# A hybrid S5 / HGRN2 block on one core: another order of weight slices, other head starts, and squares spread over 14 steps

## The chip, the cores and the metric

The kernel runs on one core of a Trainium2 chip (the other seven are idle). The metric is the device time of one execution in microseconds. Three executions of the kernel before took 1543.37, 1548.42 and 1546.52 us, median 1546.52.

## The reference

One decoder block over x of 2048 x 1024 (float32). All of it is one normalised projection, two token mixers, gates and an output projection:

```
xn   = rms_norm(x, norm_w)
proj = xn @ w_in
u_a, z_a, q_b, f_b, i_b, og_b, z_b, g_a, g_b = split(proj)
y_a  = s5_branch(u_a, z_a, ...)
y_b  = hgrn2_branch(q_b, f_b, i_b, og_b, z_b, lower_bound, norm_w)
merged = sigmoid(g_a) * (y_a @ w_proj_a) + sigmoid(g_b) * (y_b @ w_proj_b)
return rms_norm(x + merged @ w_out, final_norm_w)
```

In the HGRN2 branch a head has 128 channels: q goes through silu, f through a sigmoid with a lower bound (the forget gate), key = 1 - forget, and the recurrence is evaluated in chunks, as scores inside a chunk and a carried state between chunks. So a head can start only when its columns of q, f, i (here V) and og (here O) of the projection are complete.

## The kernel before, in words

**Two halves, Strassen products.** The rows are worked on in two halves of 1024 (a = 0 and 1), each in two blocks of 512 columns (b). The first slices are multiplied plainly (`plain`). Then `strassen(0, s0)`, the first long stage, works through 18 slices of w_in, each 256 features wide. A slice takes seven products instead of eight. One product is 12 matmuls of 128x512: four k blocks, each as high x high, low x high and high x low part (lines 445, 446, 447), because each float32 operand is split into two parts (`split`: line 119 on ScalarE makes the high part, line 120 on VectorE the low part). In the code a product is one `yield`, here called a step. The order of the steps is (i,0), then products 5 and 6 of the slice before, then (i,1) to (i,4): the last product of slice i is step 7i+7 (the very first has no predecessor). Steps are counted from 0; there are 126.

**What lies beside the steps.** `w_ops` fetches the weights of a product three steps ahead, splits them and stores the split parts to DRAM (wc) for the second half. When a block of a slice is complete its evacuation runs: `snap` copies an accumulator to SBUF on ScalarE (line 451), `total` adds another to it on VectorE (line 454). qf slices give Q and F of a head (`qf_evac`), vo slices V and O (transposed on TensorE by `turn`), zb and za slices a silu, ga and gb slices a sigmoid.

**Events.** `timed` runs a list of (step, function) pairs between the steps. `heads(a, first, every, last)` makes the events of the four heads: `hgrn_core` of a head is stepped 22 times from its start on, two blocks b alternating over 11 stages (`hgrn_block`), then a Newton iteration for the norm, then `hgrn_fin`. Its first stage makes K, KX = K*Q, the parts kh and kl, and two matmuls against ones (lines 953 and 954); stages 1 to 8 double the width of the chunk, then follow the states (st, pv) and the outputs (po). In the first half the heads start at steps 3, 38, 73 and 108, the last one with its 22 steps squeezed into 18.

**Row sums of the second half.** `norm_stats(1, b)` loads four tiles xr of 128x1024 and squares each on ScalarE with a running sum (line 191), then `newton_rsqrt` (12 small VectorE instructions) and `norm_diag` (four VectorE instructions) make a diagonal; `bcast(b)` broadcasts it by a matmul. `stats(0)` is an event at step 2, `stats(1)` one at step 8, the broadcasts are at 13 and 18. `xprep(1, k)` (36 pieces from step 20 on) prepares the X operands of the second half and stores them to DRAM.

**After the 126 steps** comes `merge_b(0)`, 20 more steps, with four loads of the w_proj_b weights (rpb, line 304; parts hpb and lpb), and then `strassen(1, s1)`, the second long stage.

**What sets the order.** TensorE's order is the order in which the code is written (`manual_schedule`). The order on ScalarE (ACT), VectorE (DVE) and in SyncE's DMA queue (SP) is set by a scheduler from the written program. Each engine works its list from front to back: an instruction that waits holds all behind it on that engine.

Of the kernel before, what the change touches and what calls it, by code (L numbers as in the profile page):

```python
# [11 lines left out]
F32 = mybir.dt.float32  # L12
# [3 lines left out]
AF = mybir.ActivationFunctionType  # L16
ALU = mybir.AluOpType
# [4 lines left out]
D = 1024  # L22
HALF = 1024
# [8 lines left out]
def hybrid_block(  # L32
# [24 lines left out]
    nc = tc.nc  # L57
    V = nc.vector
# [41 lines left out]
    def y4(name):  # L100
        return yp.tile([128, 1024], F32, name=name, tag="y")
# [13 lines left out]
    def r2(name, dt=F32R):  # L115
        return rp.tile([128, 512], dt, name=name, tag="r")
# [61 lines left out]
    def norm_stats(a, b):  # L178
        t0 = a * HALF + b * 512
        c0 = a * 8 + b * 4  # L180
        for i in range(4):
            rows = slice(t0 + i * 128, t0 + (i + 1) * 128)
            if a == 0:
                for h in range(2):
                    xr = r2(f"xr{a}{b}{i}{h}", F32)
                    nc.sync.dma_start(xr, xn[rows, h * 512 : h * 512 + 512])
                    S.activation(xr, xr, AF.Square, accum_out=ssh[:, h * 4 + i : h * 4 + i + 1])
            else:
                xr = y4(f"xr{a}{b}{i}")
                nc.sync.dma_start(xr, xn[rows, :])  # L190
                S.activation(xr, xr, AF.Square, accum_out=ssx[:, c0 + i : c0 + i + 1])
        if a == 0:
            V.tensor_tensor(ssx[:, c0 : c0 + 4], ssh[:, 0:4], ssh[:, 4:8], op=ALU.add)
        newton_rsqrt(ssx[:, c0 : c0 + 4], 4, 1.0 / D, rst[:, c0 : c0 + 4])

    def norm_diag(a, b):
        c0 = a * 8 + b * 4
# [1144 lines left out]
    def step(g, n=1):  # L1342
        for _ in range(n):
            next(g, None)
# [9 lines left out]
        for _, f in ev[i:]:  # L1354
            f()

    def heads(a, first, every=35, last=22):
        ev = []
        cores = [hgrn_core(a, h) for h in range(4)]
        fins = [hgrn_fin(a, h, None if a or h < 3 else (lambda b, y: yb_pair(a, 3, b, y))) for h in range(4)]  # L1360
        for h in range(4):
            t0 = first + every * h
            n = last if h == 3 else 22
            for s in range(22):
                ev.append((t0 + s * n // 22, lambda c=cores[h]: step(c)))
            ev.append((t0 + n - 1, lambda c=cores[h]: run(c)))
            for s in (-8 if a == 0 and h == 3 else 0, 1, 2, 3, 4):
                ev.append((t0 + n + s, lambda f=fins[h]: step(f)))
            ev.append((t0 + n + 4, lambda f=fins[h]: run(f)))
        return ev  # L1370

    def steps(ev, g, at):
        for t in at:
            ev.append((t, lambda: step(g)))
        ev.append((at[-1], lambda: run(g)))
# [10 lines left out]
    with tc.manual_schedule(engines={mybir.EngineType.PE}):  # L1386
# [37 lines left out]
        for i in range(12):  # L1424
            step(g)
            step(x0p[i // 4], 3 if i % 4 == 1 else 2)
            if i % 4 == 3:
                run(x0p[i // 4])
        run(g)
        s0 = [zz(0, "zb", 0), gt(0, 0, 0), gt(0, 1, 0), qf(0, 1), vo(0, 1), zz(0, "zb", 1), gt(0, 0, 1), gt(0, 1, 1),  # L1430
              qf(0, 2), vo(0, 2), zz(0, "za", 0), gt(0, 0, 2), gt(0, 1, 2), qf(0, 3), vo(0, 3), zz(0, "za", 1),
              gt(0, 0, 3), gt(0, 1, 3)]
        d0 = strassen(0, s0)
        g = plain(SL_VO, 1, w_vo, e_vo)
        step(g, 1)
# [10 lines left out]
        def bcast(b):  # L1446
            rb1[b] = norm_bcast(1, b, dg1[b])
# [1 line left out]
        dg1 = {}  # L1449

        def stats(b):
            norm_stats(1, b)
            dg1[b] = norm_diag(1, b)

        ev = heads(0, 3, 35, 18)
        ev += [(2, lambda: stats(0)), (8, lambda: stats(1)), (13, lambda: bcast(0)), (18, lambda: bcast(1))]
        xg = chain(*[xprep(1, k, rb1) for k in range(4)])
        steps(ev, xg, [20 + (s * 92) // 35 for s in range(36)])
        for i in range(6):
# [11 lines left out]
        d1 = strassen(1, s1)  # L1471
        step(d1)

        ev = heads(1, 17)
        bg_ = ssm_build()
        steps(ev, bg_, [8 + (s * 50) // 42 for s in range(43)])
        batches = [ssm_batch(0, b, wr4, wr4) for b in range(8)] + [ssm_batch(1, b, wr4, wr4) for b in range(2)]
# [134 lines left out]
```

## Time and profile before

| | before |
|---|---|
| three runs, median | 1546.52 us (1543.37 to 1548.42) |
| the profiled execution's own time | 1544.01 us |
| its span in the trace | 1542.2 us |
| mean granted TensorE clock | 0.984 |
| TensorE busy | 1467.2 us, 95% of the span |
| VectorE busy | 1099.2 us, 71% |
| ScalarE busy | 636.3 us, 41% |
| first long stage, steps 0 to 125 | 103.67 to about 534 us |
| merge_b(0), then start of the second long stage | about 534 to 587; from 588 us |

How to read it: a step of 12 matmuls that follow each other without a gap takes 2.72 us from start to start (0.227 us each), though the profile gives each matmul 0.39 us, since neighbours overlap. Head work on TensorE comes on top. At half of the clock the matmuls stand 0.43 us apart. A step's time in the trace is from its first matmul to that of the next step; a wait shows as a step that is longer than its instructions.

### The profile page before, as it was taken

To read this page: it belongs to the slowest core of one execution; us is meant where nothing else is said; L and a number is where in the kernel's file an instruction comes from. 1 tells how busy PE (TensorE), PEld (TensorE's weight loads), DVE (VectorE), ACT (ScalarE), POOL (GpSimd) and SP (SyncE) were. 2 spreads that over 40 slices of the span, in tenths; PEclk is the share of its full clock that TensorE was granted. 3 is DMA by queue.
4 is the path that set the end of the run, shared out by engine and by line. 5 is a ranking of instruction groups with operands and counts; after the bars stand their busy time and mean duration, and the time that the engine had idled before them with its cause. 6 is when DMAs were issued, how large, how long until landed. Compare 5 with 4: busy or idle time off the path is not lost.

```text
span 1542.2 us, 21503 instructions
## 1 busy us (share of the span) xinstructions
PE 1467.2 (95%) x7360; PEld 1206.0 (78%) x7360; DVE 1099.2 (71%) x2403; ACT 636.3 (41%) x1385; POOL 3.6 (0%) x24
## 2 busy tenths in 40 slices
PE   7997999999999989989999999999989899999997
PEld 5776788888878768868777888788768788778886
DVE  5898788788788635975665877766648977765445
ACT  7455555554554513223322445333344333532222
POOL 0000000000000000000000000000000000000000
PEclk9998999999999999999999999999989999999999
DMA  9639779887978896586669559678976963854602
GB/s 336 174 121 301 296 274 337 328 293 270 352 271 324 288 371 219 183 208 216 221 205 318 176 148 296 225 254 261 321 223 205 302 208 128 277 187 133 211 14 103
DMA packets 202141, 369.23 MB, mean 239 GB/s; under 512 B 66800, under 2 KB 76016, under 8 KB 202032
## 3 DMA queue, kind: packets, MB, share of 16 engines
q1 hardware_dynamic: 173872, 342.69, 65.8%
q10 hardware_dynamic: 28160, 25.17, 4.8%
q8 instruction: 58, 0.95, 0.3%
q14 instruction: 51, 0.42, 0.1%
HBM read 221.51 MB, written 146.28 MB: 238 GB/s over the span
## 4 chain that ended last, share of the span: by engine, by line
PE 64%; DMA 15%; DVE 14%; ACT 3%; issue 3%; SPq 1%; ACTq 0%; DVEq 0%
PE pd L445 12%; PE pd L447 12%; PE pd L446 12%; PE pf L1259 3%; PE pf L1258 3%; PE pf L1260 3%; DMA rw<-in_wi_dram 3%; PE pp L1097 2%; PE pp L1098 2%; PE pp L1096 2%; PE sc L966 1%; DMA w<-wc 1%; DVE w L120 1%; DMA y_d<-T 1%; PE pd L342 1%
## 5 line engine op out<-in xcount | busy, mean ns | idle before, releaser
L119 ACT ACTIVATE w<-rw 128x512 fp32r<-128x512 f32 x110 | 68.5, 628 | 94.4 <-PE pd L447 45.5
L1258 PE MATMUL pf<-ho,mh 128*128 128x512 f32 x256 | 100.6, 393 | 4.5 <-ACT mh L119 4.5
L1260 PE MATMUL pf<-ho,ml 128*128 128x512 f32 x256 | 100.0, 391 | 0.2 <-DVE ml L120 0.2
L1259 PE MATMUL pf<-lo,mh 128*128 128x512 f32 x256 | 99.9, 390 | 0.0
L451 ACT ACTIVATE u<-pd 128x512 f32<-128x512 f32 x80 | 47.6, 595 | 101.0 <-PE pd L447 97.2
L120 DVE TENSOR_TENSOR w<-rw,w 128x512 fp32r<-128x512 f32 x110 | 75.2, 686 | 19.5 <-ACT w L119 19.2
L454 DVE TENSOR_TENSOR u<-u,pd 128x512 f32<-128x512 f32 x80 | 54.9, 686 | 28.8 <-PE pd L447 22.0
L342 PE MATMUL pd<-xh,hw 128*128 128x512 f32 x128 | 52.4, 409 | 9.0 <-ACT hw L119 7.5
L1258 PEld LDWEIGHTS pf<-ho,mh 128*128 128x128 f32 x256 | 48.2, 188 | 14.6 <-ACT mh L119 4.9
L1260 PEld LDWEIGHTS pf<-ho,ml 128*128 128x128 f32 x256 | 48.1, 188 | 10.8 <-DVE ml L120 0.9
L1259 PEld LDWEIGHTS pf<-lo,mh 128*128 128x128 f32 x256 | 48.2, 188 | 9.7
L119 ACT ACTIVATE mh<-sgl 128x512 fp32r<-128x512 f32 x32 | 20.1, 630 | 84.9 <-DVE sgl L1204 84.9
L343 PE MATMUL pd<-xl,hw 128*128 128x512 f32 x128 | 51.0, 398 | 0.0
L344 PE MATMUL pd<-xh,lw 128*128 128x512 f32 x128 | 50.8, 397 | 0.0
L1097 PE MATMUL pp<-yl,hpa 128*128 128x512 f32 x128 | 49.9, 390 | 0.2 <-DVE yl L120 0.2
L1096 PE MATMUL pp<-yh,hpa 128*128 128x512 f32 x128 | 50.1, 392 | 0.0
L1098 PE MATMUL pp<-yh,lpa 128*128 128x512 f32 x128 | 49.8, 389 | 0.0
L1203 DVE TENSOR_TENSOR sgl<-sgl,pp 128x512 f32<-128x512 f32 x48 | 32.8, 684 | 23.3 <-PE pp L1098 23.2
L961 ACT ACTIVATE KX<-K 128x128 f32<-128x128 f32 x128 | 32.4, 304 | 38.8 <-DVE K L1004 30.1
L967 DVE COPY_PREDICATED s_buf<-masks,sc 128x256 f32<-128x256 uint8 x64 | 32.5, 508 | 20.9 <-PE sc L966 20.9
L966 PEld LDWEIGHTS sc<-Q,KX 128*128 128x128 f32 x256 | 38.5, 191 | 9.7 <-issue 3.6
L966 PE MATMUL sc<-Q,KX 128*128 128x128 f32 x256 | 39.4, 277 | 4.1 <-DVE Q L1003 3.2
(915 smaller groups left out, 4434.5 us busy)
## 6 DMA issues: line engine op xcount, KB each, us to landing
wc<-w SPq DMA_DIRECT2D x126, 512.0 KB, 3.5
w<-wc SPq DMA_DIRECT2D x126, 512.0 KB, 4.7
rw<-in_wi_dram SPq DMA_DIRECT2D x44, 512.0 KB, 5.3
sgl<-sg_d SPq DMA_DIRECT2D x48, 256.0 KB, 3.0
sg_d<-u ACTq DMA_DIRECT2D x32, 256.0 KB, 3.3
ro<-in_wo_dram SPq DMA_DIRECT2D x16, 512.0 KB, 5.2
hh<-in_xn_dram SPq DMA_DIRECT2D x32, 256.0 KB, 5.0
out_dram<-hh SPq DMA_DIRECT2D x32, 256.0 KB, 2.4
```

What stands on the lines that cost most here:

```text
L119: S.activation(hi, raw, AF.Copy)
L120: V.tensor_tensor(lo, raw, hi.bitcast(F32), op=ALU.subtract)
L445: mm(o, w[:, 0, k], xh, start=(first and k == 0), stop=False, skip_group_check=True)
L446: mm(o, w[:, 0, k], xl, start=False, stop=False, skip_group_check=True)
L447: mm(o, w[:, 1, k], xh, start=False, stop=(k == 3), skip_group_check=True)
L966: mm(ps[:, :, c, :], ch(kx, c), qp, start=True, stop=True)
L1096: mm(ps, hi[:, k, fs], yh, start=(k == 0), stop=False)
L1097: mm(ps, hi[:, k, fs], yl, start=False, stop=False)
L1098: mm(ps, lo[:, k, fs], yh, start=False, stop=(k == last))
L1258: mm(o, mh[:, ts_], hi, start=(kk == 0), stop=False)
L1259: mm(o, mh[:, ts_], lo, start=False, stop=False)
L1260: mm(o, ml[:, ts_], hi, start=False, stop=(kk == 7))
```

## The change

Three parts. (1) The squares of the second half's rows leave `stats` and become a generator `norm_stats1`, called at steps 1, 2, 4, 5, 7, 8, 10, 11, 13 and 14: call i issues load i and squares the tile that was loaded two calls before. `stats(b)` keeps only the Newton iteration and the diagonal, at steps 9 and 15 instead of 2 and 8; the broadcasts are at 12 and 18 instead of 13 and 18. (2) The slices of the first long stage stand in another order: the qf and vo slices of heads 1, 2 and 3 end later (for qf at steps 42, 70 and 98 instead of 28, 63 and 98), the za slices go to the end, zb(1) and the gates come forward. (3) `heads` takes its starts as a list; the heads of the first half start at steps 9, 43, 71 and 100 instead of 3, 38, 73 and 108, each over 22 steps. In the second half they stay at 17, 52, 87 and 122.

```
@@ -180,18 +180,23 @@
-            if a == 0:
...
-            else:
-                xr = y4(f"xr{a}{b}{i}")
-                nc.sync.dma_start(xr, xn[rows, :])
-                S.activation(xr, xr, AF.Square, accum_out=ssx[:, c0 + i : c0 + i + 1])
...
+    def norm_stats1():
+        tiles = {}
+        for i in range(10):
+            if i >= 2:
+                xr = tiles.pop(i - 2)
+                S.activation(xr, xr, AF.Square, accum_out=ssx[:, 6 + i : 7 + i])
+            if i < 8:
+                tiles[i] = y4(f"xr1{i}")
+                nc.sync.dma_start(tiles[i], xn[HALF + i * 128 : HALF + i * 128 + 128, :])
+            yield
@@ -1354,15 +1359,15 @@
-    def heads(a, first, every=35, last=22):
+    def heads(a, starts):
...
-            t0 = first + every * h
-            n = last if h == 3 else 22
+            t0 = starts[h]
+            n = 22
             for s in range(22):
-                ev.append((t0 + s * n // 22, lambda c=cores[h]: step(c)))
+                ev.append((t0 + s, lambda c=cores[h]: step(c)))
@@ -1427,9 +1432,9 @@
-        s0 = [zz(0, "zb", 0), gt(0, 0, 0), gt(0, 1, 0), qf(0, 1), vo(0, 1), zz(0, "zb", 1), gt(0, 0, 1), gt(0, 1, 1),
-              qf(0, 2), vo(0, 2), zz(0, "za", 0), gt(0, 0, 2), gt(0, 1, 2), qf(0, 3), vo(0, 3), zz(0, "za", 1),
-              gt(0, 0, 3), gt(0, 1, 3)]
+        s0 = [zz(0, "zb", 0), gt(0, 0, 0), gt(0, 1, 0), zz(0, "zb", 1), gt(0, 0, 1), qf(0, 1), vo(0, 1), gt(0, 1, 1),
+              gt(0, 0, 2), qf(0, 2), vo(0, 2), gt(0, 1, 2), gt(0, 0, 3), qf(0, 3), vo(0, 3), zz(0, "za", 0),
+              zz(0, "za", 1), gt(0, 1, 3)]
@@ -1449,11 +1454,13 @@
         def stats(b):
-            norm_stats(1, b)
+            c0 = 8 + b * 4
+            newton_rsqrt(ssx[:, c0 : c0 + 4], 4, 1.0 / D, rst[:, c0 : c0 + 4])
             dg1[b] = norm_diag(1, b)
 
-        ev = heads(0, 3, 35, 18)
-        ev += [(2, lambda: stats(0)), (8, lambda: stats(1)), (13, lambda: bcast(0)), (18, lambda: bcast(1))]
+        ev = heads(0, (9, 43, 71, 100))
+        steps(ev, norm_stats1(), [1, 2, 4, 5, 7, 8, 10, 11, 13, 14])
+        ev += [(9, lambda: stats(0)), (12, lambda: bcast(0)), (15, lambda: stats(1)), (18, lambda: bcast(1))]
@@ -1471,7 +1478,7 @@
-        ev = heads(1, 17)
+        ev = heads(1, (17, 52, 87, 122))
```

In the changed program line numbers are 5 higher from line 186 on (7 or 8 higher behind `norm_stats1`'s end in `heads` and after it).

**First place: ScalarE's list between the start of the first long stage and its fourth step.** xr are the tiles to be squared, u_10 the copy of the first slice's accumulator after its third product, V and O the transposed head-0 values. Before:

```order
L119 ACTIVATE X036h<-xb_1123 128x512
L191 ACTIVATE xr_1276,ssx<-xr_1276 128x1024
L901 ACTIVATE V_1354<-pt_1349 128x512
L191 ACTIVATE xr_1279,ssx<-xr_1279 128x1024
L119 ACTIVATE kh_1336<-KX_1334 128x256
L961 ACTIVATE KX_1334<-K_1332 128x64x2 x2
L119 ACTIVATE w_14_1_1427<-rw_14_1_1423 128x512
L119 ACTIVATE kh_1373<-KX_1371 128x256
L904 ACTIVATE O_1391<-pt_1386 128x512
L191 ACTIVATE xr_1282,ssx<-xr_1282 128x1024
L191 ACTIVATE xr_1285,ssx<-xr_1285 128x1024
L961 ACTIVATE KX_1371<-K_1369 128x64x2 x2
```

The next row there is the copy u_10_1330. With the change:

```order
L850 ACTIVATE ezb_1274<-s_10_1251 128x512
L119 ACTIVATE X036h<-xb_1123 128x512
L456 ACTIVATE u_10_1305<-pd_10_0_1238 128x512
L909 ACTIVATE O_1343<-pt_1338 128x512
L119 ACTIVATE w_14_1_1371<-rw_14_1_1367 128x512
L195 ACTIVATE xr_1253,ssx<-xr_1253 128x1024
L456 ACTIVATE u_10_1357<-pd_10_0_1238 128x512
L195 ACTIVATE xr_1278,ssx<-xr_1278 128x1024
```

The copy u_10 stood behind four squares and two conversions of head 0; now it stands ahead of the first square, and head 0's rows are gone from this stretch.

**Second place: the start of head 1 on VectorE.** K, KX, kl are head 1's, F its forget gate, Q its query, u_3 the accumulator of its qf slice to which the last product (pd_3_3) is added. Before:

```order
L925 TENSOR_SCALAR K_2480<-F_2204 128x512
L454 TENSOR_TENSOR u_3_2075<-u_3_2075,pd_3_3_2107 128x512
L1069 TENSOR_TENSOR zy_2122<-zy_2122,py_2233 128x512
L120 TENSOR_TENSOR w_11_0_2275<-rw_11_0_2273,w_11_0_2275 128x512
L877 TENSOR_TENSOR Q_2230<-Q_2230,u_3_2075 128x512
L120 TENSOR_TENSOR X103l<-xa_1936,X103h 128x512
L454 TENSOR_TENSOR s_7_2175<-s_7_2175,pd_7_1_2245 128x512
L120 TENSOR_TENSOR w_7_5_2293<-rw_7_1_2153,w_7_5_2293 128x512
L931 TENSOR_TENSOR KX_2482<-K_2480,Q_2034 128x512
L925 TENSOR_SCALAR K_2517<-F_2145 128x512
L992 TENSOR_TENSOR Q_2034<-Q_2034,F_2204 128x512
L120 TENSOR_TENSOR kl_2485<-KX_2482,kh_2484 128x512
```

With the change:

```order
L886 TENSOR_SCALAR F_2555<-F_2555,lbp 128x512
L120 TENSOR_TENSOR w_7_4_2603<-rw_7_0_2442,w_7_4_2603 128x512
L930 TENSOR_SCALAR K_2579<-F_2555 128x512
L930 TENSOR_SCALAR K_2622<-F_2505 128x512
L936 TENSOR_TENSOR KX_2581<-K_2579,Q_2432 128x512
L459 TENSOR_TENSOR u_3_2460<-u_3_2460,pd_3_3_2473 128x512
L997 TENSOR_TENSOR Q_2432<-Q_2432,F_2555 128x512
L120 TENSOR_TENSOR kl_2584<-KX_2581,kh_2583 128x512
```

and on TensorE, with the last matmuls of that product (step 42) ahead:

```order
L450 MATMUL pd_3_3_2473<-X036h,w_3_6_2486 128x512
L451 MATMUL pd_3_3_2473<-X036l,w_3_6_2486 128x512
L452 MATMUL pd_3_3_2473<-X036h,w_3_6_2486 128x512
L958 MATMUL sc_0_2587<-kh_2583,ones_r 128x512
L959 MATMUL sc_0_2587<-kl_2584,ones_r 128x512
```

Before, ten steps lay between the slice's last product and the head's first matmul; now the matmul follows the product directly, and on VectorE the addition of that product stands between KX and kl.

**Third place: SyncE's queue in merge_b(0).** rpb_5678 is the fourth load of w_proj_b, X1.. are the X operands of the second half, sgb and mb_d the gates and results of the merge. Before:

```order
L294 DMA X114h<-xo_d_1_133 128x512
L294 DMA X114l<-xo_d_1_133 128x512
L1108 DMA sgb_5657<-sg_d_13_157 128x512
L1130 DMA mb_d_3_211<-sgb_5611 128x512
L294 DMA X124h<-xo_d_2_134 128x512
L294 DMA X124l<-xo_d_2_134 128x512
L304 DMA rpb_5678<-in_wp_dram 128x1024
```

With the change:

```order
L309 DMA rpb_5530<-in_wp_dram 128x1024
L383 DMA wc_6_5063<-w_21_6_5344 128x1024
L309 DMA rpb_5584<-in_wp_dram 128x1024
L1094 DMA yl_5338<-yb_d_2_202 128x512
L1094 DMA yl_5366<-yb_d_2_202 128x512
L309 DMA rpb_5678<-in_wp_dram 128x1024
L299 DMA X100h<-xo_d_0_116 128x512
```

The fourth load stood behind 38 loads of X operands; now it stands ahead of the first of them.

## Rows read from the trace of the kernel before

**Rows 1.** The page: busy time of each engine, and the granted clock in 40 slices

```profile
PE 1467.2 (95%) x7360; PEld 1206.0 (78%) x7360; DVE 1099.2 (71%) x2403; ACT 636.3 (41%) x1385; POOL 3.6 (0%) x24
...
PEclk9998999999999999999999999999989999999999
```

**Rows 2.** Busy PE, PEld, DVE, ACT, POOL by stretch; then granted clock, DMA share, GB/s

```profile
100.00:120.00 20.00, 14.41 (x60) 10.99 (x60) 20.00 (x34) 11.47 (x21) 0.00 (x0) 0.95 0.56 181
120.00:140.00 20.00, 14.03 (x54) 11.19 (x54) 14.74 (x41) 12.17 (x27) 0.00 (x0) 0.80 0.89 311
140.00:240.00 100.00, 100.00 (x531) 82.29 (x530) 78.97 (x180) 55.16 (x130) 0.00 (x0) 1.00 0.81 294
```

**Rows 3.** Timeline of PE, steps 2 to 5: start, duration, [idle before <- releaser]

```profile
109.71 0.50 PE L445 MATMUL pd<-X002h,w 128*128 128x512 f32 x1 [0.43 <-ACT s L451]
...
118.45 0.79 PE L954 MATMUL sc<-kl,ones_r 128*128 128x512 f32 x1 [4.52 <-DVE kl L120]
...
130.37 0.79 PE L445 MATMUL pd<-X004h,w 128*128 128x512 f32 x1 [5.97 <-ACT u L451]
...
135.59 0.40 PE L445 MATMUL pd<-X000h,w 128*128 128x512 f32 x1
```

**Rows 4.** Timeline of DVE, 117 to 130 us

```profile
117.71 0.68 DVE L120 TENSOR_TENSOR kl<-KX,kh 128x512 fp32r<-128x512 f32 x1
...
121.33 0.42 DVE L941 TENSOR_TENSOR KX<-K,Q 128x256 f32<-128x256 f32 x1
121.67 0.68 DVE L387 TENSOR_TENSOR s<-rw,rw 128x512 f32<-128x512 f32 x1
...
129.66 0.17 DVE L156 TENSOR_SCALAR smi<-small 128x4 int32<-128x4 int32 x1
```

**Rows 5.** Timeline of ACT, 118 to 130 us

```profile
118.88 1.06 ACT L191 ACTIVATE xr<-xr 128x1024 f32<-128x1024 f32 x1 [2.90 <-DMA xr<-in_xn_dram]
...
128.28 1.06 ACT L191 ACTIVATE xr<-xr 128x1024 f32<-128x1024 f32 x1 [1.38 <-DMA xr<-in_xn_dram]
...
129.74 0.58 ACT L451 ACTIVATE u<-pd 128x512 f32<-128x512 f32 x1
```

**Rows 6.** Timeline of DVE at the preparation of head 1, 216 to 223 us

```profile
216.41 0.68 DVE L454 TENSOR_TENSOR u<-u,pd 128x512 f32<-128x512 f32 x1
...
222.16 0.68 DVE L120 TENSOR_TENSOR kl<-KX,kh 128x512 fp32r<-128x512 f32 x1
222.76 0.68 DVE L931 TENSOR_TENSOR KX<-K,Q 128x512 f32<-128x512 f32 x1
```

**Rows 7.** Timeline of PE, the first matmul of head 1 that reads kl

```profile
242.72 0.39 PE L954 MATMUL sc<-kl,ones_r 128*128 128x512 f32 x1
```

**Rows 8.** Timeline of PE in merge_b(0)

```profile
569.25 0.39 PE L1098 MATMUL pb<-Y031h,lpb 128*128 128x512 f32 x1
573.76 0.80 PE L1096 MATMUL pb<-Y000h,hpb 128*128 128x512 f32 x1 [4.12 <-ACT hpb L119]
...
578.80 0.39 PE L1097 MATMUL pb<-Y030l,hpb 128*128 128x512 f32 x1
```

**Rows 9.** Timeline of ACT in merge_b(0)

```profile
572.65 1.06 ACT L119 ACTIVATE hpb<-rpb 128x1024 fp32r<-128x1024 f32 x1 [27.63 <-DMA rpb<-in_wp_dram]
```

**Rows 10.** Timeline of SP's DMA issues in merge_b(0)

```profile
566.49 0.33 SPq L304 DMA_DIRECT2D rpb<-in_wp_dram  x1
```

**Rows 11.** Timeline of PE at the start of the second long stage

```profile
601.64 0.50 PE L445 MATMUL pd<-X100h,w 128*128 128x512 f32 x1 [0.45 <-ACT w L119]
```

**Rows 12.** Timeline of ACT at the start of the second long stage

```profile
604.15 0.63 ACT L880 ACTIVATE F<-u 128x512 f32<-128x512 f32 x1 [0.51 <-DVE u L454]
```

**Rows 13.** Timeline of PE after two waits in the second long stage

```profile
811.15 0.50 PE L445 MATMUL pd<-X106h,w 128*128 128x512 f32 x1 [2.27 <-DMA w<-wc]
...
987.86 1.35 PE L1068 MATMUL py<-ident,ys 128*128 128x128 f32 x4 [2.05 <-ACT ys L1064]
...
990.29 0.63 PE L445 MATMUL pd<-X115h,w 128*128 128x512 f32 x1
```

More of the change, by code (lines that the diff above doesn't have):

```diff
@@ L182, in norm_stats @@
             rows = slice(t0 + i * 128, t0 + (i + 1) * 128)
-            if a == 0:
[L184 to L187, printed above, removed]
-            else:
-                xr = y4(f"xr{a}{b}{i}")
-                nc.sync.dma_start(xr, xn[rows, :])
-                S.activation(xr, xr, AF.Square, accum_out=ssx[:, c0 + i : c0 + i + 1])
-        if a == 0:
-            V.tensor_tensor(ssx[:, c0 : c0 + 4], ssh[:, 0:4], ssh[:, 4:8], op=ALU.add)
-        newton_rsqrt(ssx[:, c0 : c0 + 4], 4, 1.0 / D, rst[:, c0 : c0 + 4])
+            for h in range(2):
+                xr = r2(f"xr{a}{b}{i}{h}", F32)
+                nc.sync.dma_start(xr, xn[rows, h * 512 : h * 512 + 512])
+                S.activation(xr, xr, AF.Square, accum_out=ssh[:, h * 4 + i : h * 4 + i + 1])
+        V.tensor_tensor(ssx[:, c0 : c0 + 4], ssh[:, 0:4], ssh[:, 4:8], op=ALU.add)
+        newton_rsqrt(ssx[:, c0 : c0 + 4], 4, 1.0 / D, rst[:, c0 : c0 + 4])
+    def norm_stats1():
[8 more added lines that the diff above has]
+            yield
     def norm_diag(a, b):
```

## The prediction

> **What bounds the kernel now.** First the page: TensorE (PE) is busy for 1467.2 of 1542.2 us and its granted clock is near full [rows 1]. So the end moves only by what makes PE wait, or run at half clock, and every part of the change has to be priced as such a wait. The table of stretches then shows where PE waits near the change: 14.41 of 20 us busy from 100 to 120 us and 14.03 of 20 at a clock of 0.80 from 120 to 140, but 100 of 100 from 140 to 240 [rows 2]. DVE, on the other hand, has not a free moment from 100 to 120 us (20.00 of 20). The timeline of PE names the waits: steps 2 to 4 start at 109.71 us, step 5 at 135.59; inside lie an idle time of 4.52 us for kl of head 0 and one of 5.97 us for the copy u of the first slice's accumulator, and half-speed matmuls behind both [rows 3]. DVE writes that kl only from 117.71 on [rows 4]. ACT copies u at 129.74, after four squares of xr tiles that hold up its list until their loads land (2.90 and 1.38 us idle ahead of two of them) [rows 5]. So the early wait has two owners: head 0's first instructions in a full DVE list, and the squares ahead of the copy in ACT's list. The change moves both.
>
> **The change part by part.** I sum against the profiled execution (1544.01 us), which lies 2.5 us under the median of the runs, 1546.52; the result is put on the median. A measurement of this kernel can tell about 0.3%, that is 4.6 us, from no change.
>
> *The early stall goes.* Steps 2, 3 and 4 take 135.59 - 109.71 = 25.88 us [rows 3]. Their 36 matmuls at 0.227 us are 8.2 us, and the head work among them (two pairs of 128x512, one of 128x256, eight transposes) 2.0, so 10.2 without waits: 15.7 are lost. With the change head 0 starts at step 9, and kl and kh leave this stretch; the copy u stands ahead of the first square. A wait of some 0.9 us for a late X operand in step 2 stays: -14.8. The squares cost 8 times 1.06 us of ACT as before, two to three steps after their load, and ACT is idle for nearly half of this stretch (11.47 and 12.17 of 20 us busy, rows 2). If the DVE list, which is full until 120 us, makes the next weights late instead, part of it comes back: -10 at worst, -15.7 at best.
>
> *Step 12.* Head 0 now runs its first stages at steps 9 to 12 together with a gate's sum. In DVE's list twenty instructions stand between the result of head 0's stage 1 and the low part of w_18_0, the first weight of step 12: eight masks and products of 128x256 with 0.34 us from start to start [rows 4], one sum of 128x512 with 0.60 [rows 6] and eleven short ones of 0.17 busy, about 0.2 from start to start [rows 4]: 2.7 + 0.6 + 2.2 = 5.5, with w_18_0 itself 6.1 us, and 0.2 for the hand-overs. In that time PE has one step of 2.72 and its small matmuls, some 3.3 us. That is a new wait of 3.0, and step 15, whose weight is loaded behind a wc store, adds some 1.0: +4.0. Ends: +1 (if DVE reaches these rows while PE is still at an earlier step) and +5.5.
>
> *Head starts 1 to 3.* Before, the first matmul that reads kl of head 1 is at 242.72 us, and kl was begun at 222.16 [rows 6, 7]: 20 us of slack. Now it follows the last product of its own slice. When that product ends, DVE does the sum u_3, then Q*F, then kl, 0.60 us each from start to start [rows 6], and 0.1 to 0.2 for each hand-over from PE to DVE and back; head 1's kl is there some 2.3 us late, and the second block's waits again for 0.45: 2.75. Head 2 starts one step behind its slice as well (70 and 71): 2.75. Head 3 has two steps (98 and 100): 1.4. Sum +6.9. Ends: +2, if kl is made ahead of the sum and the wait is hidden, and +11, if two more splits at 0.60 and a sigmoid at 0.63 [rows 6, 12] stand in front each time.
>
> *Small waits.* Stages of head 0 that share one PSUM buffer (st, po, py) now fall in with xprep's pieces at steps 28 and 32, and the last head's, no longer squeezed, in the steps before the merge. I count +3.4 for the new ones, and -1.1 for the wait on head 3's output in the merge, which its earlier end removes: +2.3, from 0 to +4.5.
>
> *The merge.* PE ends one group of matmuls at 569.25 and starts the next at 573.76, 4.12 us idle for hpb, then runs at half clock to 578.80 [rows 8]. The eleven matmuls up to there would take 2.5 us and took 5.0; with the idle time that is 6.6 us. ACT made hpb at 572.65 after 27.63 us of waiting for the load rpb [rows 9], which SP issued only at 566.49 [rows 10]. Now the load stands ahead of 38 others, and this wait goes. But DVE's list in the merge has two splits of the next stage's weights (w_2_1, w_2_2) ahead of the product that frees PE's next accumulator, and these wait for a buffer that a later tile frees: I count 2.7 for that. Net -3.9, from -6.6 to -1.
>
> *The start of the second long stage.* ACT copies u_2_5959 and makes F from it ahead of splitting w_6_0, the weight that PE needs for the next step; before, w_6_0 came first and PE was idle for 0.45 us [rows 11]. The copy has to wait for the product; then it takes 0.58, F 0.63 [rows 5, 12], the two parts of w_6_0 0.6 each, with the hand-overs 2.7 us: +2.3, from 0 to +2.9.
>
> *The clock.* New waits of 2 to 3 us may be followed by half clock. After 2.27 us idle at 811.15 the next matmul lasts 0.50, as at full clock; after 2.05 us at 987.86 the matmuls are at 0.63, the lower of the two levels, 1.2 instead of 2.4 GHz [rows 13]. So both occur at the same length of wait. A piece of eight matmuls at 0.43 instead of 0.227 us from start to start costs 1.6 to 1.7 more. I take one of the five or six new waits: +1.7, from 0 to +6.8.
>
> The Trainium skill, page "TensorE: Matmul & The Clock Gate", section "HAM oscillation — how this bites in real kernels", says that only longer idle gaps make TensorE restart at the low clock; by it the new waits would cost their own length alone and the sum would be 1.7 lower. The trace disagrees at 987.86 [rows 13], so the rows decide.
>
> Sum: -14.8 + 4.0 + 6.9 + 2.3 - 3.9 + 2.3 + 1.7 = **-1.5 us**, on the median **1545 us**. The early stall is not saved but spread: over head starts, step 12 and the start of the second stage.
>
> **The rivals.** *A: the new waits are mostly hidden.* If DVE and ACT reach the head starts with their lists empty (ACT is idle for over half of the span, rows 1), kl is made in the gap after the product and costs 2 instead of 6.9; step 12 costs 2 instead of 4 and the clock stays up. -14.8 + 2 + 2 + 2.3 - 3.9 + 2.3 = -10.1: 1536. For it: no wait at all in 100 us after the early stall, with DVE at 79% [rows 2]. Against it: the head's matmul directly behind the product cannot start before three DVE instructions.
>
> *B: the head starts cost more (slower).* Place: sc of heads 1 to 3. Each costs the 2.75 us, two other 0.60 us splits that DVE fits in ahead of kl, and a stretch of half clock (1.7): 5.7 each, 17 together, in place of 6.9 and 1.7. Sum +6.9: 1553. It decides from 4.9 us a start on, where the sum passes +4.6. For it: DVE's list is dense in the first stage (78.97 of 100 us, rows 2), and a 2 us wait is enough for the lower clock [rows 13]. Against it: the order shows only the sum between KX and kl.
>
> *C: the early stall moves instead of going.* DVE has no free time until 120 us [rows 2]; if the weight splits of steps 5 to 8, not kl, then become what PE waits for, only 7 of the 14.8 are saved: sum +6.3, 1553. Against it: those splits ran at their places while PE waited for kl and u, not for them.
>
> **How the numbers follow.** Forecast (near balance, 1541 to 1550): 0.42. A: 0.32. B: 0.19. C: 0.07. So faster by over 0.3% 0.32, within 0.3% 0.42, slower 0.26. The ends of the terms are independent; together they are about 7.5 us either way. The range 1535 to 1555 takes in A, B and C at their own values and leaves 2 in 10 to the ends beyond.
>
> **What would show it.** Right: steps 2 to 4 in about 11 us and step 5 near 121 us; no wait for kl of head 0; idle times of 2 to 3 us ahead of the sc matmuls of heads 1 and 2 (releaser DVE kl), one of about 3 at step 12 (DVE w), none for hpb in the merge, and 2 to 3 us for a weight at the start of the second stage. A shows as head starts without idle time; B as starts at 5 us with 0.63 us matmuls behind them; C as waits for w between 120 and 135 us. The later stages, whose lists have the same order, should only shift; a difference there would prove the whole account wrong.

## The result and the profile after

The changed kernel takes 1553.67 us in the median of 8 runs (1550.03 to 1558.86), the kernel before 1544.71 (8 runs, 1542.5 to 1549.89): a ratio of 1.0059, interval [1.0042, 1.0076]. It is 9 us slower, where 1.5 us faster was forecast; the size is that of rival B. The profiled execution of the change took 1550.96 us with a span of 1549.1, 6.9 more than before.

The page of the change (busy time of each engine, then the granted clock in 40 slices) answers to [rows 1] and shows nothing: the engines do the same work, PE is busy for 2.8 us more, and the rest of its longer span (6.9 us) is waiting.

```profile
PE 1470.0 (95%) x7360; PEld 1206.7 (78%) x7360; DVE 1100.1 (71%) x2403; ACT 638.7 (41%) x1385; POOL 3.9 (0%) x24
...
PEclk9999999999999999999999999999999999999999
```

The timeline of PE in the change has the first matmuls of steps 2, 3, 4 and 5 here, which answer to [rows 3] (line numbers are higher than before, as the changed program is longer):

```profile
110.67 0.50 PE L450 MATMUL pd<-X002h,w 128*128 128x512 f32 x1 [0.79 <-ACT s L456]
...
114.87 0.48 PE L450 MATMUL pd<-X003h,w 128*128 128x512 f32 x1
...
118.06 0.48 PE L450 MATMUL pd<-X004h,w 128*128 128x512 f32 x1
...
120.92 0.39 PE L450 MATMUL pd<-X000h,w 128*128 128x512 f32 x1
```

Steps 2 to 4 take 10.25 us instead of 25.88: the early stall is gone, as forecast. Further on in the same timeline stand the waits that PE has instead:

```profile
144.91 0.50 PE L450 MATMUL pd<-X000h,w 128*128 128x512 f32 x1 [2.45 <-ACT w L119]
...
250.03 0.50 PE L958 MATMUL sc<-kh,ones_r 128*128 128x512 f32 x1 [1.68 <-ACT kh L119]
251.17 0.50 PE L959 MATMUL sc<-kl,ones_r 128*128 128x512 f32 x1 [0.64 <-DVE kl L120]
...
322.15 0.71 PE L1038 MATMUL po<-V,s_buf 128*128 128x128 f32 x4 [2.87 <-DVE st L1030]
...
351.46 0.49 PE L958 MATMUL sc<-kh,ones_r 128*128 128x512 f32 x1 [1.29 <-ACT kh L119]
352.45 0.50 PE L959 MATMUL sc<-kl,ones_r 128*128 128x512 f32 x1 [0.50 <-DVE kl L120]
...
435.76 1.35 PE L1073 MATMUL py<-ident,ys 128*128 128x128 f32 x4 [1.98 <-ACT ys L1069]
...
580.31 0.47 PE L1101 MATMUL pb<-Y000h,hpb 128*128 128x512 f32 x1 [2.51 <-DVE sgb L1134]
...
611.12 0.79 PE L450 MATMUL pd<-X100h,w 128*128 128x512 f32 x1 [6.05 <-ACT w L119]
611.71 0.63 PE L451 MATMUL pd<-X100l,w 128*128 128x512 f32 x1
```

After five of these waits TensorE runs at its lower clock for a piece, after the one at 580.31 it does not. The table of stretches shows it in the granted clock (the number behind the busy times; 0.50 is the lower of the two levels):

```profile
146.40:148.90 2.50, 2.50 (x7) 1.96 (x6) 0.69 (x3) 1.58 (x4) 0.00 (x0) 0.50 0.91 364
252.10:255.00 2.90, 2.90 (x8) 2.29 (x7) 2.71 (x5) 0.63 (x1) 0.00 (x0) 0.50 0.85 300
324.60:326.60 2.00, 2.00 (x6) 1.60 (x5) 0.45 (x1) 1.28 (x8) 0.00 (x0) 0.50 1.06 404
437.40:439.40 2.00, 2.00 (x6) 1.58 (x5) 1.50 (x3) 0.87 (x3) 0.00 (x0) 0.50 0.87 341
611.80:616.00 4.20, 4.20 (x12) 3.28 (x11) 4.20 (x10) 1.46 (x3) 0.00 (x0) 0.50 0.00 0
580.50:584.00 3.50, 3.50 (x16) 2.87 (x16) 1.55 (x3) 0.00 (x0) 0.00 (x0) 1.00 1.00 332
```

Three of the waits were forecast with nearly their size: step 12 (144.91), the starts of heads 1 and 2 (250 and 351), the merge (580.31; the wait for hpb of [rows 8] is gone). Three were not, or not in their size: po of head 1 at step 62, py of head 2 at step 94, and 6 us at the start of the second long stage, where [rows 11] had 0.45.

What is behind po stands in DVE's timeline. The state products st, which PE waits for, lie between scalings of xb (xprep), and the first of these waits 3.24 us for its load:

```profile
314.10 1.11 DVE L1030 SCALAR_TENSOR_TENSOR st<-st,t,pv 128x128 f32<-128x128 f32 x3
318.45 0.75 DVE L253 SCALAR_TENSOR_TENSOR xb<-xb,nw_t,rb 128x512 f32<-128x512 f32 x1 [3.24 <-DMA xb<-in_xt_dram]
319.12 0.34 DVE L1030 SCALAR_TENSOR_TENSOR st<-st,t,pv 128x128 f32<-128x128 f32 x1
```

At py the timeline shows the same with another load: ahead of the Newton rows, which py needs, DVE waits for a weight. (This one is read from the timeline alone; no run takes that load away.)

```profile
429.34 0.69 DVE L392 TENSOR_TENSOR s<-rw,rw 128x512 f32<-128x512 f32 x1 [3.01 <-DMA rw<-in_wi_dram]
429.95 0.17 DVE L155 TENSOR_SCALAR small<-ssq 128x8 f32<-128x8 f32 x1
```

At the start of the second long stage it is ACT that waits for a load (first row: the copy u, then F, then the split of the weight), and SP issued that load at 604.35, behind the last of the X operands; before, at 594.91 (last row, of the kernel before). Counted from the merge's first matmul that is 60.1 us after and 60.5 us before: the load comes when it always came, and PE, which no longer waits for hpb, now waits here.

```profile
605.11 0.60 ACT L456 ACTIVATE u<-pd 128x512 f32<-128x512 f32 x1 [4.84 <-PE pd L452]
606.46 0.63 ACT L885 ACTIVATE F<-u 128x512 f32<-128x512 f32 x1 [0.76 <-DVE u L459]
610.44 2.19 ACT L119 ACTIVATE w<-rw 128x512 fp32r<-128x512 f32 x4 [3.35 <-DMA rw<-in_wi_dram]
```

```profile
604.35 1.01 SPq L375 DMA_DIRECT2D rw<-in_wi_dram  x2
```

```profile
594.91 0.99 SPq L370 DMA_DIRECT2D rw<-in_wi_dram  x2
```

The account of the profiled executions, each stretch between the starts of first matmuls (step 0, step 5, the merge, the first that reads X106, the last of the program):

| stretch | before | after | difference | forecast |
|---|---|---|---|---|
| step 0 to 5 | 31.91 | 16.63 | -15.3 | -14.8 |
| step 5 to the merge | 398.81 | 423.33 | +24.5 | +16.0 |
| the merge to X106 | 73.11 | 75.20 | +2.1 | -2.7 |
| X106 to the end | 926.47 | 921.44 | -5.0 | 0 |

(The forecast of the second row is 4.0 + 6.9 + 3.4 + 1.7, of the third -1.1 - 3.9 + 2.3.) The miss has its place: steps 5 to the merge. Some 2 of its 24.5 us are no loss: six matmuls of head 0 have moved there from the stretch above (74 matmuls before, 68 after) and eight of head 3 from the one below (284 and 276).

### The profile page after: what moved, and what is told of

Read it like the earlier page. It is cut to its first block, busy times and chain, and to the rows that moved or that the text cites. A ratio compares the mean times of both kernels' runs of the same rounds, so it can differ in the third digit from the quotient of the medians.

```text
span 1549.1 us, 21472 instructions
## 1 busy us (share of the span) xinstructions
PE 1470.0 (95%) x7360; PEld 1206.7 (78%) x7360; DVE 1100.1 (71%) x2403; ACT 638.7 (41%) x1385; POOL 3.9 (0%) x24
## 4 chain that ended last, share of the span: by engine, by line
PE 61%; DVE 19%; DMA 13%; ACT 3%; issue 3%; SPq 1%; ACTq 0%; DVEq 0%
PE pd L450 11%; PE pd L452 11%; PE pd L451 11%; PE pf L1263 3%; PE pf L1265 3%; PE pf L1264 3%; PE pp L1102 2%; PE pp L1103 2%; PE pp L1101 2%; DMA rw<-in_wi_dram 2%; DVE w L120 2%; DMA y_d<-T 1%; PE sc L971 1%; DMA xb<-in_xt_dram 1%; DMA yy<-y_d 1%
## 5 line engine op out<-in xcount | busy, mean ns | idle before, releaser
L1008 DVE TENSOR_TENSOR Q<-Q,t 128x256 f32<-128x256 f32 x96 | 40.7, 424 | 8.1 <-PE sc L983 8.1
```

## The experiments

Unless said otherwise an experiment is the changed kernel with the edit shown. Times are medians, ratios are to the kernel before; stretches are read as in the table above.

### Which part does what

**Squares alone.** `s0` and the heads as before, (3, 38, 73, 108) with the last in 18 steps; part 1 stays.

```
-        ev = heads(0, (9, 43, 71, 100))
+        ev = heads(0, (3, 38, 73, 108), 18)
```

> Part 1 alone: squares spread over 14 steps, stats at 9 and 15; slices and head starts as before. Theory (T): in the trace of before, PE waited 6.1 us for the copy u behind the squares and 4.7 us for kl of head 0 behind a full VectorE list; only the first goes here, with its piece at half clock, and nothing new is paid: 1536 to 1540 us. Rival (R): the whole early gain comes from starting head 0 at step 9, and the spread squares only move the wait: within 3 us of before (1542 to 1548).

1536.61 us, 0.9931 [0.9908, 0.9955]. Steps 0 to 5 take 23.47 us: PE still waits for kl of head 0 (first fence), and not for u. From step 5 to the merge it is 400.42, as before. So part 1 alone is worth 10 us. (The profiled execution, 1541.50 us, is the slowest of the six.)

```profile
118.56 0.79 PE L959 MATMUL sc<-kl,ones_r 128*128 128x512 f32 x1 [4.51 <-DVE kl L120]
```

**Squares back.** Slices and heads of the change, squares in two bunches.

```
+            for i in range(4):
+                xr = y4(f"xr1{b}{i}")
+                nc.sync.dma_start(xr, xn[r0 : r0 + 128, :])
+                S.activation(xr, xr, AF.Square, accum_out=ssx[:, c0 + i : c0 + i + 1])
...
-        steps(ev, norm_stats1(), [1, 2, 4, 5, 7, 8, 10, 11, 13, 14])
```

> Parts 2 and 3 without part 1: squares in two bunches of four in stats at steps 2 and 8, broadcasts at 13 and 18; slices and heads as in the change. T: the copy u waits behind the squares again (about 6 us and a piece of half clock, 1.7), the kl wait does not come back: 1559 to 1563 us. R (the gain is head 0's alone): within 3 us of the change, 1550 to 1556 us.

1564.49 us, 1.0120 [1.0099, 1.0141]. The wait for u comes back, and larger, since head 0 no longer shares it out (12.86 us instead of 5.97, and no wait for kl). Steps 0 to 5 take 31.46 us, as before: head 0's move gains nothing while the squares hold the copy.

```profile
130.48 0.80 PE L450 MATMUL pd<-X004h,w 128*128 128x512 f32 x1 [12.86 <-ACT u L456]
```

**Old slices, new heads.** Parts 1 and 3, `s0` as before.

> Parts 1 and 3, the slices in the order of before: heads at 9, 43, 71 and 100, but qf1 and qf2 end at steps 28 and 63 instead of 42 and 70. T: the early gain stays, the idle times for kl at heads 1 and 2 (2.75 and 2.2 us, with one piece of half clock behind) are gone, head 3's (slack of two steps as in the change) stays: 1544 to 1549 us. R: the price lies in where the heads fall against the other events (waits at steps 62 and 94, start of the second long stage), not in the slack to the slices: 1551 to 1556 us.

1555.44 us, 1.0063 [1.0040, 1.0085]; step 5 to the merge 420.19. No start wait is left at heads 1 and 2, and hardly anything is gained: 3 us of 423.33. Other waits stand there (py of head 0 at 221.15, step 32, 2.29 us, which all runs with the old slices and head 0 at step 9 have and the runs with the new order have not; po at 318.40, pv at 412.35 and 513.86 us, 2 to 3 us each), the po and the first pv with DVE waiting for a load in front, the last behind a load that ACT and DVE wait for at 508.34:

```profile
315.17 0.75 DVE L253 SCALAR_TENSOR_TENSOR xb<-xb,nw_t,rb 128x512 f32<-128x512 f32 x1 [2.57 <-DMA xb<-in_xt_dram]
...
403.49 0.69 DVE L392 TENSOR_TENSOR s<-rw,rw 128x512 f32<-128x512 f32 x1 [1.87 <-DMA rw<-in_wi_dram]
...
409.56 0.75 DVE L253 SCALAR_TENSOR_TENSOR xa<-xa,nw_t,rb 128x512 f32<-128x512 f32 x1 [2.05 <-DMA xa<-in_xt_dram]
```

(That a head needs all four of q, f, V and O to start, as said at the beginning, is too strict: with the new slices the last product of head 1's vo slice is step 49, six steps after its start. With the old slices it is step 35, and the wait at po is there all the same.)

**Heads three steps later.**

```
-        ev = heads(0, (9, 43, 71, 100))
+        ev = heads(0, (9, 46, 74, 103))
```

> The change with heads 1 to 3 three steps later (9, 46, 74, 103), slices as in the change. T: no idle time ahead of the first sc matmul of heads 1 to 3, 5 to 7 us less than the change if nothing else moves: 1546 to 1550 us. R: the waits at steps 62 and 94 only move with the heads and others take the place of those gone: 1551 to 1556 us.

1534.49 us, 0.9923 [0.9904, 0.9943]: 19 us less than the change for one tuple of numbers, three times what either expectation allowed. Step 5 to the merge falls from 423.33 to 402.78. The waits at the starts, at po (step 62) and at py (step 94) are all gone, with one of 1.18 us for po of head 1 at step 66 in their place; the wait for hpb in the merge (5.02 us) is back, the one at the second long stage is gone.

**Old slices, heads three steps later.** Both edits.

> Slices in the order of before, heads at 9, 46, 74 and 103 (three steps later than in the change). P (the place of the heads against loads and other events decides): like the run with those heads and the new slices, 1532 to 1538 us. L (the new slice order is what profits from later heads, since with the old slices the loose starts gained nothing): 1548 to 1556 us.

1537.19 us, 0.9950 [0.9930, 0.9969]; step 5 to the merge 405.84. With either order of slices the heads at 46, 74, 103 give about 404 and at 43, 71, 100 about 422. The slice order by itself is worth 3 us, for one set of starts against the new order and for the other for it; the steps of the heads are worth 14 to 21. P was right.

### The end of the stage: the place in the queue or the DMA engines

In all kernels so far the merge's first matmul and step (1,0) of the second long stage lie 66.7 to 68.6 us apart, with the wait for hpb or with the one for the weight. Either the DMA engines are full there (D), or some loads stand at bad places in SP's queue (Q).

```
-            nc.sync.dma_start(raw, wi[sl, kh])
+            (nc.scalar if a and sl == SL_VO else nc.sync).dma_start(raw, wi[sl, kh])
```

> The change, with the weight loads rw of the vo slice at the start of the second long stage issued from ScalarE's DMA queue instead of SyncE's, so that they no longer stand behind the loads of X operands. Q (the place in the queue): the 6.05 us of idle PE ahead of step (1,0) falls to under 2, the total by 4 to 8 us to 1546 to 1550. D (the DMA engines are full from the merge to there): the load comes earlier, but the X operands behind it later; PE waits for X at the next steps, and from the merge's first matmul to the first matmul that reads X106 it stays near 75 us: 1551 to 1556.

1552.58 us, 1.0052 [1.0027, 1.0078]. The 6.05 us are gone and the merge to X106 is 70.41 instead of 75.20, though three new waits of about 1 us stand in the merge; but X106 to the end is 930.14 instead of 921.44, and nothing is won.

With the heads at 46, 74, 103 the same was done for the fourth rpb, `eng=nc.scalar if a == 0 and jj == 2 else nc.sync` in `load_w`:

> Heads at 9, 46, 74 and 103, and the fourth load rpb of the merge issued from ScalarE's DMA queue. Q: the 5.18 us of idle PE ahead of hpb go and nothing comes instead: 1526 to 1530 us. D: a wait of the same size appears at the start of the second long stage, and from the merge's first matmul to X106 it stays at 72 to 75 us: 1532 to 1538, no faster than with the load in SyncE's queue.

1531.31 us, 0.9912 [0.9884, 0.9941]. D's wait appears, 5.89 us at step (1,0):

```profile
590.96 0.80 PE L450 MATMUL pd<-X100h,w 128*128 128x512 f32 x1 [5.89 <-ACT w L119]
```

And with both loads moved:

> Heads at 9, 46, 74 and 103, with both loads (the fourth rpb and rw of the vo slice) from ScalarE's queue. Q: both waits gone, 1526 to 1530 us. D: the wait moves on to the X operands of the steps behind, 1532 to 1538 us.

1525.96 us, 0.9875 [0.9848, 0.9901], the fastest of all: 21 us under before. One wait is left in this stretch:

```profile
560.50 0.47 PE L1101 MATMUL pb<-Y000h,hpb 128*128 128x512 f32 x1 [0.84 <-DVE sgb L1134]
```

The merge to X106 takes 66.37 us. So D's number, 72 to 75 us, is refuted, and the place in the queue (Q) is what can be changed: taking away one wait shows the next, and only both together are worth it. But the DMA engines were full up to step (1,0), as D has it. The table of stretches (columns as in [rows 2]), from the merge's first matmul to step (1,0) and from there to X106, first with all loads in SyncE's queue, then with the loads moved:

```profile
522.55:589.28 66.73, 60.79 (x261) 49.01 (x259) 22.49 (x35) 11.57 (x23) 0.15 (x1) 0.95 0.96 343
589.28:595.14 5.86, 5.86 (x25) 4.54 (x25) 5.86 (x12) 4.26 (x8) 0.00 (x0) 1.00 0.08 17
```

```profile
524.16:585.10 60.94, 59.41 (x262) 47.94 (x260) 28.14 (x45) 13.48 (x25) 0.15 (x1) 1.00 0.99 356
585.10:590.54 5.44, 5.44 (x26) 4.50 (x24) 2.71 (x5) 2.87 (x5) 0.00 (x0) 1.00 0.79 269
```

Up to step (1,0) the share is 0.96 and 0.99, with 22.9 and 21.7 MB moved (GB/s times us): 1.2 MB less, which at 356 GB/s is 3.4 of the 5.8 us (an estimate). Behind it the engines were nearly idle (0.08) and now work (0.79). Over both stretches the bytes are about the same, 23 MB. The moved loads (one rpb and two rw of 512 KB each; SyncE's issues in the first run, then ScalarE's in the second) came 40 to 60 us earlier, and the last X operands, which PE reads only from X106 on, landed behind the start of step (1,0):

```profile
554.27 0.33 SPq L309 DMA_DIRECT2D rpb<-in_wp_dram  x1
...
582.49 1.07 SPq L375 DMA_DIRECT2D rw<-in_wi_dram  x2
```

```profile
514.30 0.40 ACTq L309 DMA_DIRECT2D rpb<-in_wp_dram  x1
...
522.90 0.34 ACTq L375 DMA_DIRECT2D rw<-in_wi_dram  x1
...
540.41 0.37 ACTq L375 DMA_DIRECT2D rw<-in_wi_dram  x1
```

**Squares alone, both loads moved.**

> The spread squares alone (slices and heads of before) with the fourth rpb and the vo slice's rw issued from ScalarE's queue. If the region from the merge to the second long stage is bound by places in the queue, it gets about 6 us shorter here as well: 1528 to 1532 us, and from the merge's first matmul to X106 about 67 instead of 73 us. If that needed the later heads: 1535 to 1539 us.

1533.44 us, 0.9914 [0.9880, 0.9948]; the merge to X106 65.71 us. The local gain, 7.4 us, needs no later heads, but the total fell by only 3 (from 1536.61), a little short of what was expected.

### What the steps of the heads cost

From here on both loads are on ScalarE's queue, unless said otherwise. First head 1 alone at the step of the change, `heads(0, (9, 43, 74, 103))`:

> Heads at 9, 43, 74 and 103 with both loads on ScalarE's queue: head 1 alone tight behind its slice, as in the change. If the tight start costs what its idle time says (2.75 us and half clock 1.7): 1529 to 1532 us, step 62 without a wait. If the wait for po at step 62 belongs to head 1's place as well (3 us and its piece at half clock): 1533 to 1538 us. If it costs nothing: 1524 to 1527 us.

1535.26 us, 0.9934 [0.9910, 0.9958]: 9.3 us for three steps of one head. Step 5 to the merge takes 411.29 instead of 404.13. The waits are two, at the start and, 72 us later, at po; half clock follows both:

```profile
249.42 0.50 PE L958 MATMUL sc<-kh,ones_r 128*128 128x512 f32 x1 [2.32 <-ACT kh L119]
250.56 0.51 PE L959 MATMUL sc<-kl,ones_r 128*128 128x512 f32 x1 [0.64 <-DVE kl L120]
...
322.00 0.71 PE L1038 MATMUL po<-V,s_buf 128*128 128x128 f32 x4 [3.34 <-DVE st L1030]
```

The same with the old slices, so that head 1 stands 15 steps behind its qf slice:

> Slices in the order of before, heads 9, 43, 74 and 103, both loads on ScalarE's queue: head 1 at the step of the change, but 15 steps behind its qf slice. Slack theory: no start wait and no wait at step 62, steps 5 to 99 as long as with head 1 at 46 and the old slices (315 us in the trace). Place theory: no start wait, but a wait for po or py in steps 60 to 66 stays, steps 5 to 99 take 317 to 322 us.

1538.37 us, 0.9951 [0.9931, 0.9971]. No start wait, but the wait at po stays, with the same load in front of it. Step 5 to the merge is 409.78, against 405.84 for head 1 at 46 (old slices):

```profile
314.79 0.75 DVE L253 SCALAR_TENSOR_TENSOR xb<-xb,nw_t,rb 128x512 f32<-128x512 f32 x1 [3.41 <-DMA xb<-in_xt_dram]
```

```profile
318.01 0.71 PE L1038 MATMUL po<-V,s_buf 128*128 128x128 f32 x4 [2.65 <-DVE st L1030]
```

Steps 5 to 99 take 320.27 us, as the place theory expects. So of the 7.2 us that head 1's step costs (411.29 to 404.13), about 4 belong to its place (409.78 to 405.84) and the rest to its slack. The 4 are rather too few: head 0's wait at step 32, which lies ahead of head 1's start, was 1.65 us in the run at 43 and 2.51 with half clock behind it in the run at 46. Over steps 42 to 70 alone the two differences are 8.1 and 5.6 us.

**All three heads shifted by 0, 1 and 2 steps** (3 is the run at 1525.96):

> The change (heads 9, 43, 71, 100) with the fourth rpb and the vo slice's rw from ScalarE's queue: the first point of a row of four with heads 1 to 3 shifted by 0, 1, 2 and 3 steps (the last has run: 1526.0 us). Both theories expect the waits of the change in the long stage and none of 6 us at its end: 1544 to 1548 us.

> Heads 9, 44, 72 and 101 with both loads on ScalarE's queue. Slack theory: one more step (2.72 us) covers the lateness of kl (2.3 us) at heads 1 and 2, the start waits and the half clock behind them go at once: 1527 to 1534 us, and nothing more is won by a shift of 2 or 3. Place theory (where a head's late stages st, po, py meet VectorE's and ScalarE's waits for loads): the start waits go but others stay or come, 1535 to 1546 us, and the total goes down in another step at 2 or 3.

> Heads 9, 45, 73 and 102 with both loads on ScalarE's queue. Slack theory: within 3 us of a shift of 1 and of 3. Place theory: no order is expected, anything from 1525 to 1545 us, with waits at other stages than at a shift of 1.

| shift | heads | median us | ratio | step 5 to the merge |
|---|---|---|---|---|
| 0 | 43, 71, 100 | 1552.29 | 1.0026 [1.0006, 1.0045] | 422.64 |
| 1 | 44, 72, 101 | 1536.08 | 0.9940 [0.9920, 0.9960] | 409.64 |
| 2 | 45, 73, 102 | 1536.38 | 0.9932 [0.9911, 0.9956] | 405.40 |
| 3 | 46, 74, 103 | 1525.96 | 0.9875 [0.9848, 0.9901] | 404.13 |

Without a shift the run is 4 us above what both theories expected: moving the two loads won 1.4 us here. At a shift of 1 the total lies in the place theory's range; neither theory had the equal totals at 1 and 2 and the drop at 3. The first step is worth 13.0 of the 18.5 us in the stretch, and 16 of 26 in the total. It takes away most of the slack wait and, with another meeting of st and the loads, the waits at po and py as well. At a shift of 1 the second matmul of a start still waits 0.64, as in the change. The drop of the total from 2 to 3 is another matter: of its 10 us the stretch has 1.3, the merge to X106 3.7 (70.02 to 66.37) and X106 to the end 4.3, where the program is the same.

**The load taken away.** Heads as in the change; in the third `xprep(1, k)` the tile xa stands in for xb, whose load is left out, so the X operands of that k are others.

```
-        xb = y4(f"xb{a}{k}")
+        xb = xa if a == 1 and k == 2 else y4(f"xb{a}{k}")
...
+        if xb is not xa:
```

> The change with both loads on ScalarE's queue and, in the third xprep(1, k), the load of xb left out (the tile xa is used in its place, so the X operands of that k are others): VectorE then has no load to wait for between the state products st of head 1. If that wait is what holds po at step 62 (3.2 us, and a piece at half clock), it goes and the run is 4 to 7 us under the same kernel with the load (1552.3): 1545 to 1549 us. If head 1's place costs in another way, the wait at step 62 stays or another of its size comes: 1550 to 1555 us.

1547.46 us, 1.0010 [0.9991, 1.0028], 4.8 under the kernel with the load. The wait at po is gone; one for pv of 0.58 us is left. Between step 5 and the merge only 2.0 are won (420.65), since py of head 1 now waits:

```profile
335.20 1.35 PE L1074 MATMUL py<-ident,ys 128*128 128x128 f32 x4 [1.79 <-ACT ys L1070]
```

So DVE's wait for xb is what held po, and most of it comes back one stage on, with half clock behind it.

**Xprep three steps earlier** (the change itself, with its loads in SyncE's queue, `17 + (s * 92) // 35`):

> The change (heads 9, 43, 71, 100) with the 36 pieces of xprep three steps earlier (from step 17 instead of 20), so that heads and xprep stand to each other as with heads at 46, 74, 103, while the heads stay tight behind their slices. A (alignment with xprep makes the waits at steps 62 and 94): those go, the idle times for kl at the head starts stay: 1539 to 1545 us. S (the tight starts shift all that follows and so make them): they stay, 1551 to 1556 us.

1554.80 us, 1.0053 [1.0030, 1.0075]. Both theories lose half: the waits at steps 62 and 94 go, and the time stays. Head 1's start now waits 5.78 us, because ACT and DVE wait for a weight (rw) just ahead of it:

```profile
253.17 0.79 PE L958 MATMUL sc<-kh,ones_r 128*128 128x512 f32 x1 [5.78 <-ACT kh L119]
```

```profile
245.37 0.69 DVE L392 TENSOR_TENSOR s<-rw,rw 128x512 f32<-128x512 f32 x1 [2.39 <-DMA rw<-in_wi_dram]
```

**Head 0 at 6** with heads 46, 74, 103 and both loads moved:

> Heads at 6, 46, 74 and 103 with both loads on ScalarE's queue. If head 0's stages at steps 9 to 12 beside the Newton rows make the 2.8 us wait at step 12 and the piece at half clock behind it, it goes: 1520 to 1524 us. Rival: kl of head 0 is late again behind VectorE's full list, or the wait moves to another weight: 1525 to 1530 us.

1531.38 us, 0.9908 [0.9882, 0.9934]. The wait at step 12 goes (2.45 us idle in the other runs), one of 1.87 us ahead of kh of head 0 (step 9) with a piece at half clock comes. Not better than 1525.96.

## Why the prediction was wrong

1553.67 us lies inside the stated range, but on the other side of the kernel before. Where the time between step 5 and the merge went, term by term:

| term | forecast | measured |
|---|---|---|
| waits at steps 12 and 15 | +4.0 | +4.2 |
| waits at the starts of heads 1 to 3 | +6.9 | +6.7 |
| small waits, at the stages that were named (steps 27, 28, 118 to 123) | +3.4 | +4.0 |
| waits at po and py, steps 62 and 94 | 0 | +5.2 |
| small waits of the kernel before that are gone | 0 | -4.4 |
| half clock | +1.7 | +6.4 |
| matmuls moved into the stretch | 0 | some +2.4 |
| sum | +16.0 | +24.5 |

(The measured column is an estimate from the two timelines: for each pair of neighbouring matmuls the time beyond the spacing that such pairs have at full clock in these runs, as a wait where the second matmul has an idle time ahead of it, else as half clock. The waits are those of the change, half clock and matmuls the change less the kernel before.)

*The early stall goes* was right: -15.3 measured for -14.8, 1.1 of it only moved matmuls. It needed both parts: the squares alone gave half (23.47 us for steps 0 to 5), head 0's move alone nothing (31.46).

*Step 12* was right in place and size.

*Head starts 1 to 3* came as worked out: 2.75 (1.84 and 0.91 above the usual spacing), 2.2 and 1.35 against 2.75, 2.75 and 1.4, and 0.4 for the second block of head 2.

*The clock* is the term that failed by most. It was right that waits of 2 to 3 us may or may not be followed by half clock, and took one of the five or six new waits. In the change pieces stand behind four of them in this stretch (144.91, 250.03, 322.15 and 435.76): 5 to 7 matmuls each at 0.43 instead of 0.227 us, some 5 to 6 us, where 1.7 was taken. A fifth stands behind 611.12 (some 2.5 us), none behind 580.31. The rule of the Trainium skill ("TensorE: Matmul & The Clock Gate", section "HAM oscillation — how this bites in real kernels") would have left the four out, so the rows were the better guide.

*Small waits* failed in its mechanism. It looked at the heads' late stages only for a shared PSUM buffer: a DVE instruction in front that waits for a load was priced at its own 0.6 us, and its 3.24 us of waiting at nothing. So the waits at po and py (2.87 and 1.98 us idle) were not in the sum. The order had shown scalings of xb among the products st; it does not show that the load lands late. That small waits of the kernel before would go was not in the sum either, and nearly made up for it (-4.4): luck.

The experiments price the heads' steps as a whole: three steps later for the three heads is worth 18.5 us from step 5 to the merge (422.64 to 404.13). By the same estimate some 9 of them lie at the starts, with the half clock behind them, and some 8 in the late stages (st, po, py) 15 to 23 steps on.

*The merge* was right: between its 132nd and 156th matmul, around the old wait for hpb, it is 4.3 us shorter. But the gain was not kept. *The start of the second long stage* failed as *Small waits* did: 2.7 us were worked out from ACT's rows, without the load; measured 6.05 idle, and half clock behind. The place of that load in SP's queue was not followed: it comes 60 us after the merge's start in both kernels, so what PE saved at hpb it waits here.

About 5 us are missing again behind X106 (921.44 against 926.47), although the prediction said that the later stages should only shift and that a difference there would prove the account wrong. It is no larger than the scatter: X106 to the end took 921.4 to 931.8 us over all profiles of this document, with the same program behind X106, and the change has the shortest. In the change the first wait of head 0 of that half has shrunk (0.16 instead of 3.18 us), while a later one has grown to 2.70; the same 250 matmuls take 47.8 instead of 49.3 us. The other 3.5 lie scattered over 850 us. Why moving the two loads won 8.5 us in one kernel, 3 in another and 1.4 in a third is left open: one profile of each does not tell a scatter of some microseconds behind X106 from a give-back.

*Rival B* gave 1553 and named heads 1 to 3. That its size fits is luck: it had 17 us at the starts, measured are some 9 with the half clock; no further splits stood ahead of kl, and the rest came from the late stages and the second long stage. *Rival A* and *C* did not come about: C's weights of steps 5 to 8 were in time.

## What to carry to other kernels

A list that is worked in order has to be priced with the loads that its instructions wait for, not with their durations: at the three waits that the prediction did not have, or not in their size, what stood between PE and its next matmul was a DVE or ACT instruction that waited for a load. So where background work with loads is mixed into a chain that PE waits for, try its start at several neighbouring steps before judging an idea: three steps decided between 9 us lost and 12 won. And where two loads stand one behind the other in a queue, moving one only shows the wait for the next: move both, and ask which of the transfers ahead PE needs by then.

## What was not expected of the hardware

In the merge the DMA share is 0.95 to 1.05 and 336 to 390 GB/s, which looked like a limit of the transfers; the table of stretches of the change shows it (columns as in [rows 2]):

```profile
545.00:560.00 15.00, 15.00 (x67) 12.39 (x66) 4.34 (x6) 2.25 (x4) 0.00 (x0) 1.00 0.97 350
560.00:575.00 15.00, 14.68 (x65) 11.83 (x64) 5.78 (x8) 0.63 (x1) 0.00 (x0) 1.00 1.05 390
575.00:590.00 15.00, 12.49 (x56) 10.03 (x55) 5.55 (x9) 1.15 (x2) 0.15 (x1) 1.00 0.95 336
```

Yet with these loads issued from the other queue (up to 40 to 60 us earlier, as shown above) the stretch to X106 was 6 to 7 us shorter (72.59 to 66.37, 73.15 to 65.71 and 75.20 to 67.91). A share near 1 did say that the DMA engines were full up to step (1,0): they still are (0.99). It did not say that all the bytes ahead of PE's next matmul were needed by then, nor that the engines were nearly idle just behind it (0.08).
